# DeltaNet stage of a hybrid trunk: the k heads of both groups first, one triangular solve for all eight heads, merges by pairs

## The chip, the cores and the metric

The kernel runs on one core of a Trainium2 chip. The metric is the device time of one execution in microseconds; lower is better. Three executions of the kernel before took 1593.81, 1595.70 and 1596.45 us (median 1595.7).

## What is computed

The reference is a decoder trunk of two layers over 512 positions of width 1024. Layer 0 mixes with a gated DeltaNet, layer 1 with a Conformer convolution; behind each come a cross attention (4 heads) into 256 memory rows and a squared-ReLU MLP of width 4096, with an RMS norm ahead of each part. Only the DeltaNet stage matters here (8 heads of dimension 128; i and j run over a chunk's positions):

```python
proj = h @ w_in                                   # q, k, v, z, b, a
qkv = silu(causal_depthwise_conv(qkv, w_conv))    # width 4
q, k = l2_normalize(q) * 128 ** -0.5, l2_normalize(k)
beta = sigmoid(b);  g = -exp(a_log) * softplus(a + dt_bias);  g_cum = cumsum(g)
decay[i, j] = exp(g_cum[i] - g_cum[j])            # for i >= j
lower = strict_lower((k * beta) @ k.T * decay)
u, w = triangular_solve(eye + lower, [v * beta, k * beta * exp(g_cum)])
# over the chunks: v_new = u - w @ S;  o = q_dec @ S + (q @ k.T * decay) @ v_new
#                  S = S * exp(g_last) + k_dec.T @ v_new
out = (rms_norm(o) * out_norm * silu(z)) @ w_out
```

## The kernel before, in words

The 512 positions are cut into four blocks of 128, so that every head has four lower triangular 128x128 matrices whose inverse U is needed.

**Projections.** Each fp32 product is three matmuls of fp32r parts (L220 to L222; for z L251 to L253): a weight is split into `wh`, which ACT casts (L204), and `wl`, which DVE subtracts (L72). SyncE loads the weights in halves of 128x1024 into three buffers; three split buffers let the splits run ahead. Most tensors of 128x512 live in one pool of slots; larger ones of 128x1024 for the solve live in a pool `fsp` of three.

**The order of the work.** The stage is a list of *mains*, each 12 projection matmuls, and a table of *side steps*: `S.at(main, rank, step)` says behind which main a step is written. `DN_ORDER` sets the order of the projections. Mains 0 to 3 are the gates and the first k head; before, k of heads 0 to 3 stands at mains 4 to 9, then q at 10 to 17, z at 18 to 25, v at 26 to 33; the second group of four heads follows from 34 to 65 in the same order, and from 66 to 81 come the keys and values of the first cross attention ("K", "V"). A scheduler then builds each engine's queue from what was written. Each engine takes its queue in order.

**The steps of a head**, with the names that the profile shows:
- `decay_in`: POOL multiplies `gi` = tri_le times g (L72), ACT casts `gih` (L257), DVE subtracts `gil`. `decay`: PE sums it into `dt` (L402, L403), ACT takes the exponential (L405), POOL multiplies by `tri_le`. `gsum` (L395 to L397) is the first matmul of it.
- `ev_k`, `ev_q`, `ev_v` call `conv_head`: DVE evicts a projection to `cv`, ACT scales the first tap (L415), the other three taps are DVE multiply-adds (L75), or ACT `cvq` (L419) and a POOL add: none of k's is on POOL, one of q's, all three of v's (`CONV_K`, `CONV_Q`, `CONV_V`). Then ACT's `silu` (L426).
- `k2`: PE transposes k (`kt`, L440) and multiplies the Gram matrix (`G`, L444); ACT squares and copies (L446, L448); DVE multiplies G by the decay into `bt`, and POOL scales bt by `s_all`. `q2`, `q3`: the product of q and k (`ai`, L466) and sums of squares.
- `fs_in`: ACT copies the 32x32 diagonal blocks of bt into `DB`, four copies a head (L493).
- The solve. `fs_begin`: POOL sets `X` to the identity, DVE transposes DB into `FT`. `fs_steps`: 31 times, a product `fst` and a subtraction from X on DVE (L72); this inverts the diagonal blocks, in the free dimension and for all blocks at once. `fs_end`: transposes `TB` and `UB` (L517, L518).
- The merges make U of the whole block from the inverses of the diagonal blocks. `mg_pre`: POOL clears tiles. `mg_a`: ACT copies TB into `x0` (L537, four a head), POOL copies UB into `u0`. `mg_w` (L546) and three steps `mg_y` (L558; the last one is in `mg_end`): matmuls "mg" of PE, an ACT copy, a DVE addition.
- `norm_k`, `v2` (transposes `vt` of v, L583), then `rec`: 12 steps of the recurrence for each group of four heads; `o_gate`, `o_norm` and `head_out`, and the output projection "do".

Before, the solve is done once for each group of four heads; DB has 32 columns, of which a group fills 16, so POOL clears it first. `FS` = ((20, 9), (50, 8)) starts the solves at mains 20 and 50 and spreads them over 9 and 8 mains; `MG` = (32, 63) places the merges, `REC` = (39, 68) the recurrences.

Of the kernel before, what the change touches and what calls it, by code (L numbers as in the profile page):

```python
# [14 lines left out]
P = 128  # L15
# [25 lines left out]
def tile_trunk(ctx, tc, xT, memT, prm_d, adt_d, bdw_d, w_ab, w_kq, w_v, w_z, w_dno, w_pw1, w_pw2,  # L41
# [285 lines left out]
    class DeltaNet:  # L327
        def __init__(self, norm):
            self.n, self.xs = norm, norm.xs
            for n, s in ((64, "abt"), (32, "beta"), (32, "g"), (96, "egd"), (32, "sek"), (32, "nk"),  # L330
                         (32, "s_all"), (32, "sdec"), (32, "s_neg"), (32, "sdec_neg"), (32, "ssq"), (4, "tok")):
                setattr(self, s, keepc(n, s))
            for s in ("GI", "DtM", "KT", "Kt", "Ai", "QT", "BT", "U", "VT", "VB", "Z", "OG", "ps", "M"):
                setattr(self, s, {})
            self.DB, self.fs = {}, {}
            self.S = [None, None]
# [71 lines left out]

        def conv_head(self, ps, ti, npool):
            raw = wp.tile([P, 542], F32, tag="cv", name=nm("cv"), bufs=NCV)  # L410
            pool.memset(raw[:, 0:3], 0.0)
            tt(dve, raw[:, 3:515], ps, self.n.rb, ALU.mult)
            w = [pc("w_conv", ti * 4 + j) for j in range(4)]
            a = slot(s="cva")
            act.activation(a, raw[:, 0:512], AF.Copy, scale=w[0])  # L415
# [69 lines left out]
        def fs_in(self, h):  # L485
            gq, bt, n = h // 4, c4(self.BT[h]), h % 4 * 4
            if gq not in self.DB:
                self.DB[gq] = fsp.tile([P, 1024], F32, tag="fs", name=nm("DB"))
                pool.memset(self.DB[gq], 0.0)
            db = self.DB[gq].rearrange("p (i n) -> p i n", n=32)  # L490
            for b in range(4):
                bs = slice(32 * b, 32 * b + 32)
                act.copy(db[bs, :, n:n + 4], bt[bs, :, bs].rearrange("p c i -> p i c"))  # L493

        def fs_begin(self, gq):
# [4 lines left out]
            dve.transpose(out=FT, in_=self.DB.pop(gq))  # L500
            self.fs[gq] = FT, X

        def fs_steps(self, gq, j0, j1):
            B3, X3 = [t.rearrange("p (i j) -> p i j", j=32) for t in self.fs[gq]]
            for j in range(j0, min(j1, 31)):
# [6 lines left out]

        def fs_end(self, gq):
            X = self.fs.pop(gq)[1]
            UB = fsp.tile([P, 1024], F32, tag="fs", name=nm("UB"))
            TB = fsp.tile([P, 1024], F32, tag="fs", name=nm("TB"))
            dve.transpose(out=TB, in_=X.rearrange("p (i j) -> p j i", j=32))  # L517
            dve.transpose(out=UB, in_=X)  # L518
            self.fs[gq] = UB.rearrange("p (i n) -> p n i", n=32), TB.rearrange("p (i n) -> p n i", n=32)

# [10 lines left out]
        def mg_a(self, h):  # L531
            UBv, TBv = self.fs[h // 4]
            u0, x0, bt = self.M[h]
            n = slice(h % 4 * 4, h % 4 * 4 + 4)
            for b in range(4):
# [6 lines left out]
        def mg_w(self, h):  # L542
            u0, x0, bt = self.M[h]
            ps = psum("mg")
            for c in range(4):
                pe.matmul(c4(ps)[:, c, 0:96], bt[:, c * P:(c + 1) * P], c4(x0)[:, c, 0:96], start=True, stop=True)  # L546
            w = slot(s="w")
            act.activation(c4(w)[:, :, 0:96], c4(ps)[:, :, 0:96], AF.Copy, scale=-1.0)
            self.M[h] = u0, u0, w, 1

        def mg_y(self, h):
            u0, y, w, n = self.M[h]
            ps = psum("mg")
# [9 lines left out]
            self.M[h] = u0, y, w, n + 1  # L563

# [5 lines left out]
        def ev_v(self, h):  # L570
            self.VT[h] = self.conv_head(self.ps.pop(("v", h)), 16 + h, CONV_V)

# [533 lines left out]
    at = {}  # L1106
# [203 lines left out]
CONV_K, CONV_Q, CONV_V = 0, 1, 3  # L1310
DEC1 = (37, 43)
K2 = (13, 12, 16, 17, 43, 44, 47, 46)
Q2 = (16, 18, 20, 21, 46, 48, 48, 51)
FS = ((20, 9), (50, 8))
MSTEP = (0, -1)
MG = (32, 63)
V2 = (4, 3)
MGAIN = 4
HO = 76
REC = (39, 68)  # L1320
MEM = 53
# [97 lines left out]
```

## Time and profile before

| | us |
|---|---|
| median of three executions | 1595.7 |
| profiled execution | 1596.47 |
| its span | 1594.8 |
| PE busy in it | 1545.7 |
| DVE busy | 919.2 |
| ACT busy | 661.9 |
| POOL busy | 275.3 |

The span is the time from the first to the last recorded instruction; the mean granted clock of TensorE was 0.983. A line of the timeline has start, duration, engine, source line, operation, "out<-in" by the program's names, the shape and, in brackets, the idle time just before with what ended it. In a table of windows each engine's busy time comes with its count, then the granted clock (PEclk, 1 is full), the DMA engines' busy share and GB/s. Matmuls overlap, so their durations sum to more than their starts lie apart.

### The profile page before, as it was taken

Reading aid. Unit: us, or ns where it says so; the run is one execution under the profiler, and the core shown is the slowest. Engines: PE = TensorE matmul, PEld = TensorE weight load, DVE = VectorE, ACT = ScalarE, POOL = GpSimd, SP = SyncE. Lnnn points to the kernel's source line nnn. Section 1 sums busy time; section 2 is a strip of 40 time slices with the busy share of each in tenths; the row PEclk is TensorE's granted clock in tenths of the full one; section 3 lists DMA queues with packets and bytes.
Section 4 is the critical chain, followed back from the end, with each engine's and each line's share of the span. In section 5 each row is a group of like instructions: output and inputs, shape, how many; then the busy total and the mean of one; then the engine's idle time right before and its main releaser. Section 6 shows DMA issues by size and latency. Waiting matters only on the chain.

```text
span 1594.8 us, 19977 instructions
## 1 busy us (share of the span) xinstructions
PE 1545.7 (97%) x7864; PEld 1310.7 (82%) x7864; DVE 919.2 (58%) x1304; ACT 661.9 (42%) x1014; POOL 275.3 (17%) x314
## 2 busy tenths in 40 slices
PE   9998997899999999999999999999999999999997
PEld 6777886798888888888888889888888888888897
DVE  6886878566455444343445599974445443444443
ACT  6656573745344443241324321264434442323332
POOL 1526333502111100000021316102112000000002
PEclk9999999799999999999999999999999999999999
DMA  5121113153222222322322422252213223322321
GB/s 179 67 76 57 53 40 106 43 183 106 93 66 66 86 100 93 106 93 92 104 95 93 145 80 78 76 170 95 79 40 106 93 92 98 101 93 96 103 93 54
DMA packets 47614, 147.09 MB, mean 92 GB/s; under 512 B 6304, under 2 KB 11040, under 8 KB 47520
## 3 DMA queue, kind: packets, MB, share of 16 engines
q1 hardware_dynamic: 47520, 145.81, 27.5%
q8 instruction: 62, 1.02, 0.3%
q14 instruction: 32, 0.26, 0.0%
HBM read 142.38 MB, written 2.10 MB: 91 GB/s over the span
## 4 chain that ended last, share of the span: by engine, by line
PE 83%; DVE 8%; ACT 3%; POOL 2%; issue 2%; SPq 1%; DMA 1%; DVEq 0%; ACTq 0%; POOLq 0%
PE dn L220 7%; PE dn L221 7%; PE dn L222 7%; PE up L220 7%; PE up L221 7%; PE up L222 7%; DVE ca L75 4%; PE q L220 2%; PE xo L221 2%; PE q L221 2%; PE q L222 2%; PE xo L222 2%; PE xo L220 2%; PE h L221 2%; PE pw L220 2%; PE pw L221 2%
## 5 line engine op out<-in xcount | busy, mean ns | idle before, releaser
L204 ACT CAST wh<-raw 128x1024 fp32r<-128x1024 f32 x248 | 260.3, 1051 | 706.8 <-PE dn L221 191.4
L72 DVE TENSOR_TENSOR wl<-raw,wh 128x1024 fp32r<-128x1024 f32 x248 | 313.8, 1266 | 126.6 <-ACT wh L204 120.7
L220 PE MATMUL up<-xh,wh 128*128 128x512 f32 x512 | 200.2, 391 | 0.0
L222 PE MATMUL up<-xh,wl 128*128 128x512 f32 x512 | 199.2, 389 | 0.0
L221 PE MATMUL up<-xl,wh 128*128 128x512 f32 x512 | 199.2, 389 | 0.0
L220 PE MATMUL dn<-uh,wh 128*128 128x512 f32 x448 | 174.3, 389 | 0.0
L221 PE MATMUL dn<-ul,wh 128*128 128x512 f32 x448 | 174.3, 389 | 0.0
L222 PE MATMUL dn<-uh,wl 128*128 128x512 f32 x448 | 174.3, 389 | 0.0
L72 DVE TENSOR_TENSOR h<-dn,h 128x512 f32<-128x512 f32 x56 | 41.9, 748 | 170.4 <-PE dn L222 170.4
L75 DVE SCALAR_TENSOR_TENSOR rl<-up,rb 128x512 f32<-128x512 f32 x64 | 44.2, 691 | 156.9 <-PE up L222 156.9
L72 POOL TENSOR_TENSOR tap<-ident,prm 128x512 f32<-128x512 f32 x45 | 60.7, 1380 | 330.8 <-PE up L222 263.8
L220 PEld LDWEIGHTS up<-xh,wh 128*128 128x128 f32 x512 | 96.1, 188 | 20.4 <-issue 0.5
L221 PEld LDWEIGHTS up<-xl,wh 128*128 128x128 f32 x512 | 96.1, 188 | 20.2 <-issue 0.5
L222 PEld LDWEIGHTS up<-xh,wl 128*128 128x128 f32 x512 | 96.1, 188 | 20.1
L222 PEld LDWEIGHTS dn<-uh,wl 128*128 128x128 f32 x448 | 84.1, 188 | 17.5
L220 PEld LDWEIGHTS dn<-uh,wh 128*128 128x128 f32 x448 | 84.1, 188 | 17.5
L221 PEld LDWEIGHTS dn<-ul,wh 128*128 128x128 f32 x448 | 84.1, 188 | 17.4
L72 POOL TENSOR_TENSOR sq<-sq,sq 128x512 f32<-128x512 f32 x30 | 49.9, 1664 | 252.5 <-ACT sq L295 167.8
L75 DVE SCALAR_TENSOR_TENSOR ca<-x,prm,ca 128x512 f32<-128x512 f32 x90 | 81.8, 910 | 2.1
L220 PE MATMUL h<-xh,wh 128*128 128x512 f32 x192 | 77.6, 404 | 1.9 <-ACT xh L288 1.9
L221 PE MATMUL h<-xl,wh 128*128 128x512 f32 x192 | 76.0, 396 | 0.6 <-DVE xl L75 0.6
L222 PE MATMUL h<-xh,wl 128*128 128x512 f32 x192 | 75.7, 394 | 0.0
(322 smaller groups left out, 3211.1 us busy)
## 6 DMA issues: line engine op xcount, KB each, us to landing
raw<-w_up SPq DMA_DIRECT2D x64, 512.0 KB, 3.4
raw<-w_dn SPq DMA_DIRECT2D x64, 512.0 KB, 3.4
raw<-w_pw SPq DMA_DIRECT2D x24, 512.0 KB, 3.6
raw<-w_kq SPq DMA_DIRECT2D x16, 512.0 KB, 3.7
raw<-w_k SPq DMA_DIRECT2D x16, 512.0 KB, 3.7
raw<-w_vv SPq DMA_DIRECT2D x16, 512.0 KB, 3.6
raw<-w_q SPq DMA_DIRECT2D x16, 512.0 KB, 3.5
raw<-w_o SPq DMA_DIRECT2D x16, 512.0 KB, 3.5
```

Source lines behind the costliest of these rows:

```text
L72: e.tensor_tensor(out=o, in0=a, in1=b, op=op)
L75: dve.scalar_tensor_tensor(out=o, in0=a, scalar=s, in1=b, op0=op0, op1=op1)
L204: act.copy(h, raw)
L220: pe.matmul(ps, wh, xh, start=first, stop=False)
L221: pe.matmul(ps, wh, xl, start=False, stop=False)
L222: pe.matmul(ps, wl, xh, start=False, stop=last)
```

## The change

All eight k heads are projected first (mains 2 to 17), then v of the first group at 18 to 25, q at 26 to 33, z at 34 to 41, and v, q, z of the second group at 42 to 65. There is one DB, whose 32 columns the eight heads fill (so it isn't cleared), and one solve, from main 23 over 9 mains. The decays of heads 4 to 7 come at mains 11 to 15 in place of 37 to 45. The merges go by pairs of heads, a pair every three mains from main 32, each with its own `mg_pre` one main ahead. In the merges w is written over bt, and y over x0. The v heads of the second group are convolved in the pool of the solve, whose tiles are free by then. `K2`, `Q2`, `V2` and `HO`, which place the steps named alike, move with their inputs. The diff, cut:

```diff
@@ DeltaNet.__init__
-            self.DB, self.fs = {}, {}
+            self.DB = self.fs = None
@@ conv_head, ev_v
-        def conv_head(self, ps, ti, npool):
+        def conv_head(self, ps, ti, npool, a=None):
...
-            a = slot(s="cva")
+            a = slot(s="cva") if a is None else a
...
-            self.VT[h] = self.conv_head(self.ps.pop(("v", h)), 16 + h, CONV_V)
+            a = None
+            if h >= 4:
+                if h % 2 == 0:
+                    self.VP = fsp.tile([P, 1024], F32, tag="fs", name=nm("VT"))
+                a = self.VP[:, h % 2 * 512:h % 2 * 512 + 512]
+            self.VT[h] = self.conv_head(self.ps.pop(("v", h)), 16 + h, CONV_V, a)
@@ fs_in, fs_begin, fs_end
-            gq, bt, n = h // 4, c4(self.BT[h]), h % 4 * 4
-            if gq not in self.DB:
-                self.DB[gq] = fsp.tile([P, 1024], F32, tag="fs", name=nm("DB"))
-                pool.memset(self.DB[gq], 0.0)
-            db = self.DB[gq].rearrange("p (i n) -> p i n", n=32)
+            bt, n = c4(self.BT[h]), h * 4
+            if self.DB is None:
+                self.DB = fsp.tile([P, 1024], F32, tag="fs", name=nm("DB"))
+            db = self.DB.rearrange("p (i n) -> p i n", n=32)
...
-            dve.transpose(out=FT, in_=self.DB.pop(gq))
-            self.fs[gq] = FT, X
+            dve.transpose(out=FT, in_=self.DB)
+            self.fs = FT, X
...
@@ mg_a, mg_w, mg_y
-            n = slice(h % 4 * 4, h % 4 * 4 + 4)
+            n = slice(h * 4, h * 4 + 4)
...
-            w = slot(s="w")
+            w = bt
...
-                y = slot(s="y")
+                y = x0
...
@@ the table of side steps
+    f0, nf = FS
+    S.at(f0, 5, D.fs_begin)
+    for i in range(nf):
+        S.at(f0 + i, 6, D.fs_steps, i * 31 // nf, (i + 1) * 31 // nf)
+    S.at(f0 + nf, 0, D.fs_end)
+    for h in range(8):
+        S.at(MGP[h], 5, D.mg_pre, h)
+        S.at(MG[h], 1, D.mg_a, h)
+        for j, f in enumerate((D.mg_w, D.mg_y, D.mg_y, D.mg_end)):
+            S.at(MG[h] + MGLAG + j, 1, f, h)
     for gq in range(2):
-        f0, nf = FS[gq]
-        S.at(f0, 5, D.fs_begin, gq)
-        for i in range(nf):
-            S.at(f0 + i, 6, D.fs_steps, gq, i * 31 // nf, (i + 1) * 31 // nf)
-        S.at(f0 + nf, 0, D.fs_end, gq)
-        S.at(f0 + 1, 7, D.norm_k, gq)
-        for i in range(4):
-            h = 4 * gq + i
-            m = MG[gq] + i * MSTEP[gq] // 2
-            S.at(m, 1, D.mg_a, h)
-            S.at(f0 + nf - 4 + i, 5, D.mg_pre, h)
-            for j, f in enumerate((D.mg_w, D.mg_y, D.mg_y, D.mg_end)):
-                S.at(m + 1 + j, 1, f, h)
+        S.at(f0 + 1 + gq, 7, D.norm_k, gq)
         for c in range(4):
-            S.at(max(at["v", 4 * gq + 3] + V2[gq], f0 + nf), 3, D.v2, gq, c)
+            S.at(at["v", 4 * gq + 3] + V2[gq], 3, D.v2, gq, c)
@@ the numbers
-DN_ORDER = (("k", 0), ("q", 0), ("z", 0), ("v", 0), ("k", 1), ("q", 1), ("z", 1), ("v", 1))
+DN_ORDER = (("k", 0), ("k", 1), ("v", 0), ("q", 0), ("z", 0), ("v", 1), ("q", 1), ("z", 1))
...
-DEC1 = (37, 43)
+DEC1 = (11, 13)
...
-FS = ((20, 9), (50, 8))
-MSTEP = (0, -1)
-MG = (32, 63)
+FS = (23, 9)
+MGP = (31, 31, 34, 34, 37, 37, 40, 40)
+MG = (32, 32, 35, 35, 38, 38, 41, 41)
+MGLAG = 1
...
-REC = (39, 68)
+REC = (41, 66)
```

How this moves instructions. **POOL**, behind the first decays. The names: gi_442 and dt_515 to dt_545 are of heads 0 to 3. Before:

```order
L72 TENSOR_TENSOR gi_442<-tri_le,g 128x512
L72 TENSOR_TENSOR dt_515<-dt_515,tri_le 128x512
L72 TENSOR_TENSOR dt_521<-dt_521,tri_le 128x512
L72 TENSOR_TENSOR dt_539<-dt_539,tri_le 128x512
L72 TENSOR_TENSOR dt_545<-dt_545,tri_le 128x512
L411 MEMSET cv_1198 128x3
L72 TENSOR_TENSOR cva_551<-cva_551,cvq_553 128x512
```

and in the changed order, where gi_557, gi_563 and dt_626 are of heads 4 to 7 and bt_602 is a scaled Gram matrix:

```order
L72 TENSOR_TENSOR dt_515<-dt_515,tri_le 128x512
L72 TENSOR_TENSOR dt_521<-dt_521,tri_le 128x512
L72 TENSOR_TENSOR dt_539<-dt_539,tri_le 128x512
L72 TENSOR_TENSOR gi_557<-tri_le,g 128x512
L72 TENSOR_TENSOR dt_545<-dt_545,tri_le 128x512
L411 MEMSET cv_1011 128x3
L72 TENSOR_TENSOR gi_563<-tri_le,g 128x512
L411 MEMSET cv_1065 128x3
L72 TENSOR_TENSOR bt_602<-bt_602,s_all 128x512
L72 TENSOR_TENSOR dt_626<-dt_626,tri_le 128x512
```

The products gi of heads 4 to 7, which were far behind, now stand between and behind the dt products of heads 0 to 3.

**ACT**, around the last copies into DB. Before, the first solve's last copies (DB_666, of the fourth head's bt_775):

```order
L575 ACT_TABLE_LOAD
L575 ACTIVATE nk<-sek 128x16
L426 ACT_TABLE_LOAD
L426 ACTIVATE cva_793<-cva_793 128x512
L493 COPY DB_666<-bt_775 32x32x4 x4
L204 CAST wh_859<-raw_699 128x1024
L578 ACTIVATE s_neg<-s_all 128x16
L578 ACTIVATE sdec_neg<-sdec 128x16
L468 ACTIVATE sqq_914<-cva_793 128x512
L204 CAST wh_938<-raw_805 128x1024
L204 CAST wh_995<-raw_857 128x1024
```

In the changed order the last copies are of the seventh and eighth head, and the first v heads' taps (cva_1014, cvq_1016 and so on) stand among them:

```order
L426 ACT_TABLE_LOAD
L426 ACTIVATE cva_941<-cva_941 128x512
L492 COPY DB_721<-bt_929 32x32x4 x2
L415 ACTIVATE cva_1014<-cv_1011,prm 128x512
L419 ACTIVATE cvq_1016<-cv_1011,prm 128x512
L419 ACTIVATE cvq_1019<-cv_1011,prm 128x512
L419 ACTIVATE cvq_1022<-cv_1011,prm 128x512
L492 COPY DB_721<-bt_929 32x32x4 x2
L204 CAST wh_1031<-raw_880 128x1024
L426 ACTIVATE cva_1014<-cva_1014 128x512
L492 COPY DB_721<-bt_989 32x32x4 x4
L204 CAST wh_1095<-raw_956 128x1024
```

Behind these rows FT can be transposed; before, that takes 16 copies of four heads, now 32 of eight.

**PE**, at the merges. Before, the first group's merges (mg_1322 and on, with x0 and bt as operands) stand in one row of four heads:

```order
L222 MATMUL h_1264<-xh_166,wl_1145 128x512
L546 MATMUL mg_1322<-x_218_1044,bt_627 128x96 x4
L546 MATMUL mg_1329<-x_227_1080,bt_592 128x96 x4
L546 MATMUL mg_1336<-x_238_1126,bt_740 128x96 x4
L546 MATMUL mg_1343<-x_247_1163,bt_775 128x96 x4
L220 MATMUL h_1370<-xh_138,wh_1214 128x512
L221 MATMUL h_1370<-xl_140,wh_1214 128x512
```

and the second group's far behind, next to the sum mssq of the memory's squares:

```order
L546 MATMUL mg_2615<-x_530_2449,bt_1961 128x96 x4
L719 MATMUL mssq_2622<-msq_2426,ones 128x256 x2
L546 MATMUL mg_2666<-x_510_2369,bt_1844 128x96 x4
L546 MATMUL mg_2673<-x_519_2407,bt_2022 128x96 x4
L558 MATMUL mg_2680<-u_529_2448,w_2620 96x96 x4
L220 MATMUL h_2720<-xh_138,wh_2528 128x512
```

In the changed order the first pair (mg_1481, mg_1487) stands behind the last q projection of group 0, and the second pair (mg_1650, mg_1656) behind the first z steps; the first pair's further steps and z projections lie between the two pieces:

```order
L222 MATMUL h_1402<-xh_166,wl_1235 128x512
L545 MATMUL mg_1481<-x_302_1369,bt_649 128x96 x4
L545 MATMUL mg_1487<-x_304_1377,bt_602 128x96 x4
L466 MATMUL ai_1493<-cva_1360,cva_418 128x128 x4
L251 MATMUL z_1512<-wh_1297,xh_138 128x512
...
L557 MATMUL mg_1638<-x_302_1369,bt_649 32x32 x4
L557 MATMUL mg_1644<-x_304_1377,bt_602 32x32 x4
L545 MATMUL mg_1650<-x_342_1555,bt_712 128x96 x4
L545 MATMUL mg_1656<-x_344_1563,bt_764 128x96 x4
L480 MATMUL ssq_1662<-ones,sqq_1617 128x1 x4
L251 MATMUL z_1514<-wh_1398,xh_146 128x512
```

The eight heads' merges are spread over the mains 33 to 45, with projections between the steps, and nothing of a second group is left behind them.

More of the change, by code (lines that the diff above doesn't have):

```diff
@@ L493, in fs_in, with fs_begin @@
                 act.copy(db[bs, :, n:n + 4], bt[bs, :, bs].rearrange("p c i -> p i c"))
-        def fs_begin(self, gq):
+        def fs_begin(self):
             X = fsp.tile([P, 1024], F32, tag="fs", name=nm("X"))
@@ L499, in fs_begin, with fs_steps @@
             FT = fsp.tile([P, 1024], F32, tag="fs", name=nm("FT"))
-            dve.transpose(out=FT, in_=self.DB.pop(gq))
-            self.fs[gq] = FT, X
-        def fs_steps(self, gq, j0, j1):
-            B3, X3 = [t.rearrange("p (i j) -> p i j", j=32) for t in self.fs[gq]]
+            dve.transpose(out=FT, in_=self.DB)
+            self.fs = FT, X
+        def fs_steps(self, j0, j1):
+            B3, X3 = [t.rearrange("p (i j) -> p i j", j=32) for t in self.fs]
             for j in range(j0, min(j1, 31)):
@@ L511, in fs_steps, with fs_end @@
                 tt(dve, X3[:, w:32, 0:w], X3[:, w:32, 0:w], t3, ALU.subtract)
-        def fs_end(self, gq):
-            X = self.fs.pop(gq)[1]
+        def fs_end(self):
+            X = self.fs[1]
             UB = fsp.tile([P, 1024], F32, tag="fs", name=nm("UB"))
@@ L546, in mg_w @@
                 pe.matmul(c4(ps)[:, c, 0:96], bt[:, c * P:(c + 1) * P], c4(x0)[:, c, 0:96], start=True, stop=True)
-            w = slot(s="w")
+            w = bt
             act.activation(c4(w)[:, :, 0:96], c4(ps)[:, :, 0:96], AF.Copy, scale=-1.0)
-            self.M[h] = u0, u0, w, 1
+            self.M[h] = u0, u0, w, x0, 1
         def mg_y(self, h):
-            u0, y, w, n = self.M[h]
+            u0, y, w, x0, n = self.M[h]
             ps = psum("mg")
@@ L1310 @@
 CONV_K, CONV_Q, CONV_V = 0, 1, 3
-DEC1 = (37, 43)
-K2 = (13, 12, 16, 17, 43, 44, 47, 46)
-Q2 = (16, 18, 20, 21, 46, 48, 48, 51)
-FS = ((20, 9), (50, 8))
-MSTEP = (0, -1)
-MG = (32, 63)
-V2 = (4, 3)
+DEC1 = (11, 13)
+K2 = (13, 12, 14, 15, 16, 17, 19, 20)
+Q2 = (30, 31, 33, 35, 54, 56, 58, 60)
+FS = (23, 9)
+MGP = (31, 31, 34, 34, 37, 37, 40, 40)
+MG = (32, 32, 35, 35, 38, 38, 41, 41)
+MGLAG = 1
+V2 = (8, 7)
 MGAIN = 4
-HO = 76
-REC = (39, 68)
+HO = 73
+REC = (41, 66)
 MEM = 53
```

6 lines of the change are left out of this document (3 added, 3 removed).

## The prediction

> **What bounds the kernel now.** I read the page's first lines, then the table of time windows cut at three events of the program, then the list of PE's waits, then the timelines of the engines that those waits name.
>
> ```profile
> span 1594.8 us, 19977 instructions
> PE 1545.7 (97%) x7864; PEld 1310.7 (82%) x7864; DVE 919.2 (58%) x1304; ACT 661.9 (42%) x1014; POOL 275.3 (17%) x314
> ...
> PE 83%; DVE 8%; ACT 3%; POOL 2%; issue 2%; SPq 1%; DMA 1%; DVEq 0%; ACTq 0%; POOLq 0%
> ```
>
> PE is busy for 97% of the span, so all but some 50 us of the kernel is matrix work, and 83% of the chain that ended last is PE. A change that leaves every matmul in place can only move the rest: the idle time of PE and the time in which PE ran at less than its full clock. Both have to be looked for in the DeltaNet stage, the only one that is changed. Four PE events divide it.
>
> ```profile
> 44.07 0.31 PE L395 MATMUL gsum<-g,ones 128*128 128x32 f32 x2
> ...
> 136.41 7.04 PE L546 MATMUL mg<-x,bt 128*128 128x96 f32 x32 [4.93 <-ACT x L537]
> ...
> 373.73 0.39 PE L220 MATMUL do<-oh,wh 128*128 128x512 f32 x1
> ...
> 374.41 0.39 PE L220 MATMUL do<-oh,wh 128*128 128x512 f32 x1
> ```
>
> The columns are start, duration, engine, line and operation. At 44.07 comes the first matmul of the decays, at 136.41 the first merge (of heads 0 to 3), at 373.73 the output projection. The second group's first merge is at 280.58 and comes up below as the end of a wait. Up to 44.07 and behind 373.73 PE has the same rows in both programs, so the change decides one number: when "do" starts. The windows between the events:
>
> ```profile
> core 0: us, PE busy (x) PEld busy (x) DVE busy (x) ACT busy (x) POOL busy (x), PEclk, DMA share, GB/s
> 44.10:136.40 92.30, 81.06 (x403) 67.14 (x402) 77.58 (x130) 54.71 (x90) 38.72 (x54) 0.98 0.23 75
> 136.40:280.60 144.20, 129.16 (x761) 112.34 (x761) 108.88 (x195) 82.86 (x148) 58.81 (x90) 0.94 0.19 63
> 280.60:373.70 93.10, 89.39 (x612) 81.88 (x613) 59.30 (x86) 55.15 (x98) 24.28 (x32) 0.89 0.34 114
> ...
> 44.10:92.40 48.30, 41.98 (x217) 34.61 (x216) 36.31 (x50) 34.02 (x58) 24.38 (x35) 0.96 0.20 66
> 280.60:310.50 29.90, 26.18 (x145) 23.08 (x146) 15.44 (x20) 25.59 (x51) 21.10 (x30) 0.67 0.11 36
> ```
>
> In the first window PE stands idle for 92.30 - 81.06 = 11.2 us, in the second for 15.0, in the third for 3.7. The clock column adds a second loss: (1 - 0.94) x 144.2 = 8.7 us in the second window and (1 - 0.89) x 93.1 = 10.2 us in the third, nearly all of the latter in its first 29.9 us (0.67 of full clock). Behind the first merge the stage loses 15.0 + 3.7 + 8.7 + 10.2 = 37.6 us. The waits say what for:
>
> ```profile
> PE mg L546 <- POOL msq L72: 11.2, 1, 11.2
> PE mg L546 <- ACT x L537: 5.3, 2, 4.9
> ```
>
> The columns are total, times and longest. The 11.2 us end with the first merge of the second group. The view names POOL's sum of squares, but that stands on another tile; what the merge needs is the second solve, whose last DVE transpose ends late (a solve takes 41 us, below). So two waits for a solve, and the slow clock behind each, are what this stage loses.
>
> **The change, first part: when the one solve can start.** It starts with the transpose FT, which needs the diagonal blocks of all eight heads, copied by ACT (DB, 4 copies a head). ACT takes its queue in order, so its queue up to the last DB copy is what I sum. Before, FT started at 92.49.
>
> ```profile
> L493 ACT COPY DB<-bt 32x128 f32<-32x128 f32 x16 | 6.7, 418 | 4.8 <-POOL bt L72 4.6
> L204 ACT CAST wh<-raw 128x1024 fp32r<-128x1024 f32 x4 | 4.2, 1040 | 1.9 <-PE h L221 1.9
> L415 ACT ACTIVATE cva<-cv,prm 128x512 f32<-128x512 f32 x5 | 3.6, 725 | 0.1
> L426 ACT ACTIVATE cva<-cva 128x512 f32<-128x512 f32 x5 | 3.2, 631 | 5.8 <-DVE cva L75 5.7
> L419 ACT ACTIVATE cvq<-cv,prm 128x512 f32<-128x512 f32 x4 | 2.9, 714 | 0.0
> L426 ACT ACT_TABLE_LOAD x2 | 2.6, 1283 | 0.0
> L446 ACT ACTIVATE sqk<-kt 128x512 f32<-128x512 f32 x4 | 2.4, 589 | 0.0
> L448 ACT COPY kt<-kt 128x512 f32<-128x512 f32 x4 | 2.3, 572 | 0.0
> L405 ACT ACTIVATE dt<-dt 128x512 f32<-128x512 f32 x4 | 2.0, 593 | 0.0
> L257 ACT CAST gih<-gi 128x512 fp32r<-128x512 f32 x3 | 1.8, 616 | 2.1 <-POOL gi L72 2.1
> ```
>
> These are ACT's groups between 44.1 and 92.4; the number behind the comma is the mean of one in ns. The first row where both orders still agree on ACT is the cast that ends at 51.98:
>
> ```profile
> 50.93 1.05 ACT L204 CAST wh<-raw 128x1024 fp32r<-128x1024 f32 x1 [1.91 <-PE h L221]
> ```
>
> From there to the last DB copy the changed order holds 32 DB copies (13.4 us), 5 casts (5.2), 8 squares and 8 copies of kt (9.3), 7 table loads (9.0), 8 exponentials (4.7), 4 casts of gi (2.5), 7 first taps (5.1), 7 silu (4.4) and 6 further taps (4.3): 58 us as recorded. Records overlap: the groups of the window sum to 36.5 us where its row says 34.02 busy, so 58 become 54. With no idle time FT starts at 52 + 54 = **106**; with ACT as busy as in that window (34.02 of 48.30) at 52 + 54/0.704 = **129**. What I see between: in the changed order the POOL products gi of heads 4 to 7 stand behind the dt products of heads 0 to 3, and ACT's cast of each gi waits at the head of its queue.
>
> ```profile
> L72 POOL TENSOR_TENSOR gi<-tri_le,g 128x512 f32<-128x512 f32 x3 | 5.4, 1828 | 0.0
> ...
> 53.16 6.37 POOL L72 TENSOR_TENSOR dt<-dt,tri_le 128x512 f32<-128x512 f32 x4 [4.80 <-ACT dt L405]
> ```
>
> One dt product takes 6.37 / 4 = 1.59 us; the first gi, behind three, ends at 53.16 + 3 x 1.59 + 1.83 = 59.8, when ACT has come to its cast at 51.98 + 0.73 + 4 x 0.59 = 55.1: 4.7 us of wait. The second pair meets two dt products and no third; I take 3.5. Behind the cast stand the taps, the silu and the DB copies, so all are late by it. With 2 us for smaller waits (bt on POOL): 52 + 54 + 8 + 2 = **116**.
>
> **Second part: how long the solve takes.** The number of DVE steps is that of one solve of before: the tile had 32 columns, of which 16 were used. The rows are from DVE's timeline, from the window of the steps' tile fst (us, DVE busy and count, clock, DMA share, GB/s) and from DVE's groups, of the solve and (taps) of the stretch ahead of it.
>
> ```profile
> 92.49 1.25 DVE L500 STREAM_TRANSPOSE FT<-DB 128x1024 f32<-128x1024 f32 x1 [1.70 <-ACT DB L493]
> 115.81 0.39 DVE L72 TENSOR_TENSOR X<-X,fst 128x231 f32<-128x231 f32 x1
> 117.67 1.37 DVE L72 TENSOR_TENSOR X<-X,fst 128x220 f32<-128x220 f32 x1
> 131.96 1.93 DVE L517 STREAM_TRANSPOSE TB<-X 128x1024 f32<-128x1024 f32 x1
> ...
> 92.00:136.40 44.40, 26.18 (x62) 1.00 0.25 83
> ...
> L72 DVE TENSOR_TENSOR wl<-raw,wh 128x1024 fp32r<-128x1024 f32 x7 | 8.5, 1212 | 0.0
> L72 DVE TENSOR_TENSOR cv<-h,rb 128x512 f32<-128x512 f32 x4 | 2.7, 676 | 0.1
> L75 DVE SCALAR_TENSOR_TENSOR cva<-cv,prm,cva 128x512 f32<-128x512 f32 x11 | 11.8, 1074 | 3.4 <-POOL cva L72 3.2
> ```
>
> Before, it ran from 92.49 to 133.89, 41.4 us. The window row counts the steps alone: 62 in 26.18 us. The changed order puts beside them 5 weight splits (6.1), 4 conv evictions (2.7), 6 taps (6.4) and 2 products of q, priced as evictions (1.4), and there are FT and TB (3.2) and some 0.035 us between two steps (2.2): **48 us**. So TB ends at 116 + 48 = 164. Then ACT copies the blocks into x0, and the first merge can go:
>
> ```profile
> 135.02 6.72 ACT L537 COPY x<-TB 32x128 f32<-32x128 f32 x16
> ```
>
> That is 0.42 each. The merge of the first head needs 4 of them, 1.7 us: **166**, with 154 + 2 = 156 and 179 as bounds. PE itself isn't late by then: its work up to there grows by about 5.3 us (below).
>
> The two X steps above stand 2 us apart and take 0.39 and 1.37: the second began beside a POOL add. The Trainium skill, page "SBUF — State Buffer", section "Who interferes with whom", says that DVE's second pair of ports is shared with GpSimd under an exclusive lock; the two rows agree, though on average a step took 26.18 / 62 = 0.42. By that rule the three further POOL adds beside the new solve cost 1 us each, and the sum would be 3 us higher, 1592. The terms above leave it out.
>
> **Third part: from the first merge to the output projection.** Before: 373.73 - 136.41 = 237.3 us. Two things come off.
>
> ```profile
> 55.02 1.06 PE L444 MATMUL G<-cva 128*128 128x128 f32 x8
> 55.83 0.47 PE L220 MATMUL h<-xh,wh 128*128 128x512 f32 x1
> ...
> 315.72 1.97 PE L583 MATMUL vt<-ident,cva 128*128 128x128 f32 x16
> ```
>
> Work moved ahead of the first merge: both orders have 276 projection matmuls there. The change adds 8 decays of 512 columns at 0.227 (three do matmuls in 374.41 - 373.73), 16 Gram matmuls at 0.203 (four, as 8 records, from 55.02 to 55.83), and 16 + 16 transposes at about 0.11 (16 in 1.97 less the drain of the last): 1.8 + 3.2 + 3.5. It takes away 8 q·k matmuls and 8 sums at 0.2: 3.2. Net **5.3 us**.
>
> Losses that go: of the 37.6 us, the second solve, its 11.2 us of wait and the half clock behind it have no place in the new order, because all U are there long before the second group's recurrence. What remains: a half clock behind the new first wait (3.4 us, as 136.4 to 143.2 had it), some 2 us in the recurrences, and 1.3 us elsewhere, because a pair's merge steps now have one projection step of 2.7 us between them. That is 6.7 in place of 37.6, **30.9** off; the bounds of what remains are 3 (little but the clock) and 13 (with the 9.9 us that the clock lost in 280.6 to 310.5). So 237.3 - 5.3 - 30.9 = 201.1, and do starts at 166 + 201.1 = 367.1, **6.6 us sooner**. DVE has more room than before behind the merge, by one solve. The moved norm_k, the reused w and y tiles and the v heads in another pool I take at nothing: they add no instruction to PE or ACT, and the copy into w waits for the matmuls that read bt anyway, since it reads their result. The reuse frees slots, so it may gain too; I allow 3 us either way, about PE's idle time in the third window.
>
> The profiled execution is 1596.47 us, 1.7 above its span, and 0.8 above the median 1595.7. 1596.5 - 6.6 = 1589.9; against the median **1589**.
>
> **The rivals.** (a) *ACT is the whole bound and hardly waits.* For: after 52 its queue is dense in the new order. Against: ACT was idle for 30% of the first half. FT at 106 to 110 gives 1579 to 1583. (b) *The long wait before the first merge keeps PE slow.* PE now stands for about 30 us around the merge, far more than before; behind the second merge the clock was 0.67 for 29.9 us, 9.9 us lost, against 3.4 in my sum. Then 6.5 of the 6.6 us are gone: about 1595.6, no change. The Trainium skill, "TensorE: Matmul & The Clock Gate", Part 1, has full rate return after about 3.4 us of sustained work; the stretch behind 136.4 agrees, the 29.9 us behind 280.6 don't, where PE had gaps. By that rule this rival would not come. (c) *The solve starts too late: slower.* Its place is ACT's queue ahead of the last DB copy. Every us there moves the first merge and with it do by one. The gain is gone when FT starts at 116 + 6.6 = 122.6. With ACT's idle share of before it starts at 129: 6.4 us slower, 1602. For it: new waits of ACT for POOL, and 8 heads in one queue. Against: fewer q and z rows of ACT stand between. That the change doesn't make one solve can be left out: the order has one FT, one TB and one UB.
>
> **How the numbers follow.** Forecast (1583 to 1592.5) 0.40; bigger gain (a) 0.17; no change (b) 0.19; slower (c) 0.24. About 0.2%, 3.2 us, is what a measurement can tell from no change. Faster is 0.40 + 0.17 = 0.57, same 0.19, slower 0.24. The low end is (a) with 3 us of remaining losses in place of 6.7: 1577; the high end is (c) with 1 us more: 1603.
>
> **What would show it.** FT near 116, TB's end near 164, first merge near 166 and do near 367; PE without the 11.2 us wait; DVE busy some 30 us less than 919.2; a PE wait of over 20 us around the first mg, on ACT x or on the casts. FT beyond 122 with do late says (c); a low clock for more than 7 us behind the merge says (b). If PE waits in the merges or recurrences for more than 7 us, my third part is wrong.

## The result, and the profile after

**No change.** Twelve executions of the changed kernel have a median of 1595.85 us (1594.75 to 1597.31) beside 1596.03 us (1592.50 to 1597.30) for twelve of the kernel before: a ratio of 1.0004, 95% interval 0.9997 to 1.0011 (estimated from all executions of both, here and below, so not the quotient of the two medians). The forecast was 6.6 us less. The single executions of either kernel lie up to 5 us apart, and their mean granted clock goes with them (the kernel before: 1592.6 us at 0.987, 1597.0 at 0.983, in one set of runs), so of all that follows only differences over some 2 us are read from times; the rest is read from one trace of each kernel, between two of its own events.

The changed kernel's page, its first lines:

```profile
span 1594.1 us, 19919 instructions
PE 1543.3 (97%) x7864; PEld 1304.3 (82%) x7864; DVE 893.1 (56%) x1239; ACT 663.3 (42%) x1014; POOL 273.4 (17%) x310
```

DVE does 26 us less, as one solve less should make it. PE is as busy as it was, and as long. The four events in its timelines, of PE and DVE:

```profile
44.43 0.31 PE L395 MATMUL gsum<-g,ones 128*128 128x32 f32 x2
...
169.28 1.10 PE L545 MATMUL mg<-x,bt 128*128 128x96 f32 x8 [2.10 <-issue]
...
373.60 0.39 PE L220 MATMUL do<-oh,wh 128*128 128x512 f32 x1
```

```profile
116.47 1.25 DVE L499 STREAM_TRANSPOSE FT<-DB 128x1024 f32<-128x1024 f32 x1 [0.65 <-ACT DB L492]
...
165.30 2.06 DVE L516 STREAM_TRANSPOSE TB<-X 128x1024 f32<-128x1024 f32 x1
```

FT starts where the working put it (116), TB ends at 167.4 in place of 164, the first merge comes at 169.3 in place of 166, and "do" at 373.6 in place of 367: 0.1 us before where it was. So the stage's two parts, ahead of and behind the first merge, changed as forecast in kind: the first merge is 33 us later and all that follows it 33 us shorter. The windows show both:

```profile
core 0: us, PE busy (x) PEld busy (x) DVE busy (x) ACT busy (x) POOL busy (x), PEclk, DMA share, GB/s
...
116.50:167.40 50.90, 33.52 (x138) 26.96 (x137) 44.84 (x86) 21.39 (x34) 14.71 (x19) 0.77 0.18 61
44.40:169.30 124.90, 96.15 (x444) 77.66 (x442) 100.66 (x169) 81.55 (x137) 60.88 (x90) 0.88 0.17 55
169.30:373.60 204.30, 202.15 (x1333) 179.03 (x1333) 120.56 (x181) 112.96 (x198) 66.04 (x88) 0.99 0.29 95
...
116.50:143.00 26.50, 18.27 (x66) 13.85 (x65) 25.04 (x42) 15.95 (x25) 9.51 (x11) 0.87 0.29 97
143.00:169.30 26.30, 15.26 (x73) 13.16 (x73) 21.71 (x47) 7.30 (x14) 5.84 (x10) 0.68 0.07 21
```

Behind the first merge PE is idle for 2.2 us of 204.3 at 0.99 of its clock: hardly anything is left to gain there, and the 11.2 us wait is gone. Ahead of it PE is idle for 28.75 us (before: 11.2). In the last 26.3 us ahead of the merge it is busy for 15.3 at 0.68 of the clock. PE's waits, the largest three of the whole execution (the third lies behind "do"), say for whom:

```profile
PE ai L466 <- ACT cva L426: 12.1, 2, 8.6
PE h L222 <- DVE wl L72: 3.9, 2, 2.4
PE K L222 <- DVE wl L72: 3.8, 2, 3.6
```

The longest of PE's waits are not for the solve. PE stands for the silu of two q heads, whose products with k ("ai") are next in its queue. And DVE, in the middle of the solve, stands for PE. DVE's waits between 90 and 172, the first two:

```profile
DVE wl L72 <- ACT wh L204: 8.5, 3, 4.3
DVE ssq L81 <- PE ssq L480: 3.8, 1, 3.8
```

The chain of work, followed back from the first merge, crosses over (start, duration, what):

```profile
150.37 0.39 DVE fst L72
150.76 0.66 DVE cva L75
151.42 0.30 DVE X L72
151.72 0.67 DVE cva L75
...
152.42 0.64 ACT cva L426
...
153.10 2.07 PE ai L466 x8
155.17 1.50 PE ssq L480 x8
156.67 0.64 PE h L220
...
161.85 0.79 PE ssq L480 x8
162.63 1.80 PE vt L587 x16
...
167.19 2.10 issue
169.28 0.77 PE mg L545 x5
```

A tap of q lies among the solve's steps in DVE's queue (151.72); ACT's silu waits for it, PE's "ai" for the silu (8.6 us). PE has stood long enough for its clock to fall, so the 12 projection matmuls that follow take 5.2 us (156.67 to 161.85) in place of 2.8. Behind them comes the sum of squares of q, and for that DVE stops between two solve steps, from 158.8 to 162.7. **PE waits for DVE's queue, and DVE's queue then waits for PE.**

Where did the gain go? Every microsecond from "gsum" to "do" is one of three: PE idle, the half of its busy time at half clock that is lost, or the work at full clock. Worked out from PE's records and the clock of each trace:

| from gsum to do | elapsed | PE idle | lost at half clock while busy | work at full clock |
|---|---|---|---|---|
| before, to the first merge | 92.3 | 11.2 | 1.7 | 79.4 |
| before, from there to do | 237.3 | 18.8 | 13.9 | 204.7 |
| changed, to the first merge | 124.9 | 28.8 | 9.9 | 86.2 |
| changed, from there to do | 204.3 | 2.2 | 1.7 | 200.5 |

Lost time fell by 28.8 us behind the merge and grew by 25.7 ahead of it; the work grew by 2.6 in all. PE has the same 1775 matmul records in both kernels; why they take 2.6 us more was not taken apart.

### The profile page after: what moved, and what is told of

The parts are those of the page before. It is cut to its first block, busy times and chain, and to the rows that moved or that the text cites. A ratio compares the mean times of both kernels' runs of the same rounds, so it can differ in the third digit from the quotient of the medians.

```text
span 1594.1 us, 19919 instructions
## 1 busy us (share of the span) xinstructions
PE 1543.3 (97%) x7864; PEld 1304.3 (82%) x7864; DVE 893.1 (56%) x1239; ACT 663.3 (42%) x1014; POOL 273.4 (17%) x310
## 4 chain that ended last, share of the span: by engine, by line
PE 82%; DVE 11%; ACT 3%; issue 2%; POOL 1%; DMA 0%; DVEq 0%; SPq 0%; POOLq 0%; ACTq 0%
PE dn L220 7%; PE dn L222 7%; PE dn L221 7%; PE up L220 7%; PE up L222 7%; PE up L221 7%; DVE ca L75 4%; PE q L220 2%; PE xo L221 2%; PE q L222 2%; PE q L221 2%; PE xo L222 2%; PE xo L220 2%; DVE wl L72 2%; PE pw L220 2%
## 5 line engine op out<-in xcount | busy, mean ns | idle before, releaser
L220 PE MATMUL h<-xh,wh 128*128 128x512 f32 x192 | 81.2, 423 | 6.1 <-ACT wh L204 3.7
```

What stands on the lines that cost most here:

```text
L220: pe.matmul(ps, wh, xh, start=first, stop=False)
```

## The experiments

Theory A was that PE and DVE wait for each other ahead of the first merge, and that the lost time can be had back if PE has other work there. Its rivals are named in the expectations. "From gsum" means that the start of "gsum" in the same trace is subtracted; in the changed kernel TB then ends at 122.9, the first merge is at 124.9 and do at 329.2.

**1. The sums of squares of q later** (e1, and once more beside the changed kernel, e14 and e13).

```diff
-        S.at(Q2[h] + 1, 3, D.q3, h)
+        S.at(Q2[h] + 1 if h >= 4 else 36 + h // 2, 3, D.q3, h)
```

> The changed kernel, with the sums of squares of q of heads 0 to 3 written behind mains 36 and 37 in place of 31 to 36. Theory A (PE and DVE wait for each other: DVE, in the middle of the solve, stands 3.8 us for PE's ssq, while PE stands for taps that are queued behind solve steps): the end of TB moves from 167.4 to about 163.5, the first merge from 169.3 to 166 or 167, where PE itself comes free; the 8 sums (1.6 us) come later instead; do starts 0.8 to 2.2 us sooner, 1594 to 1595. Theory B (the 3.8 us are slack of DVE that something else would fill): TB ends at 167 and the time stays at 1595.9 or rises.

> The kernel with the sums of squares of q later, once more. Its trace had do 1.8 us sooner after the first decay than the changed kernel's, but its median of 11 runs was not faster. If the gain is real and the spread hid it: 1 to 2.5 us below the changed kernel beside it. If PE's slow clock gives it back in most executions: within 1 us of it or above.

> The changed kernel once more, as the measure for the two runs beside it: 1595 to 1597, within 0.1% of the kernel before.

The three events in the trace of e1:

```profile
43.35 0.31 PE L395 MATMUL gsum<-g,ones 128*128 128x32 f32 x2
...
160.57 2.05 DVE L516 STREAM_TRANSPOSE TB<-X 128x1024 f32<-128x1024 f32 x1
...
164.39 1.10 PE L545 MATMUL mg<-x,bt 128*128 128x96 f32 x8 [2.10 <-issue]
```

TB ends at 119.3 from gsum, 3.7 us sooner, the first merge comes 3.8 sooner (121.0), and do 1.8 sooner (327.4) in the one trace and 2.1 in the other (the sums themselves now come behind the merge, where the work grows from 200.5 to 202.5 us): DVE's wait for PE was 3.7 us of the solve, as theory A has it, and theory B falls. The time doesn't settle it. The ratio to the kernel before was 1.0005 (0.9996 to 1.0014) in the first set and 0.9999 (0.9990 to 1.0008) in the second, where the changed kernel beside it had 1.0006 (0.9998 to 1.0015); the medians were 1596.8, then 1594.3 beside 1596.4. Executions of this kernel reach from 1592.6 to 1597.9. Whether the 2 us arrive in the median stays open.

**2. The q products behind the merge, the merges later, and both.** These three are read together: e2, e5 and e3 (e12 is e3 again).

```diff
-Q2 = (30, 31, 33, 35, 54, 56, 58, 60)
+Q2 = (36, 37, 38, 39, 54, 56, 58, 60)
```

> The changed kernel, with the q products and sums of heads 0 to 3 behind the first merges (mains 36 to 39 in place of 30 to 35). Theory A: PE no longer waits 12.1 us for q's silu and reaches the first merge some 15 us early, but waits there for TB, which ends near 164; the q work (3.2 us) now follows the merge. The two cancel: do at 373 to 374, 1595.5. Theory C (PE's waits for q's taps are what makes the first merge late): the time falls by 8 us or more, below 1588.

```diff
-MGP = (31, 31, 34, 34, 37, 37, 40, 40)
-MG = (32, 32, 35, 35, 38, 38, 41, 41)
+MGP = (35, 35, 38, 38, 41, 41, 44, 44)
+MG = (36, 36, 39, 39, 42, 42, 45, 45)
...
-REC = (41, 66)
+REC = (45, 66)
```

> The changed kernel, with merges and first recurrence four mains later, as in the run that gained, but with the q products left at mains 30 to 35. Theory A (before the merge PE stands for q's taps, not for TB, so a later merge alone gives it nothing to do): 1593 to 1596.5, and PE's two waits of 12 us for q's silu stay. Rival (the merges' place alone made the gain): 1589 or less.

The third has the second diff, and Q2 = (37, 38, 39, 40, 54, 56, 58, 60).

> The changed kernel, with the merges and the first recurrence four mains later and the q products behind the first merge. Theory A: while the solve ends, PE does four more mains (11 us) that it did behind the merge before; with 3.2 us of q work moved the other way do starts about 8 us sooner: 1588. Theory D (DVE is full from 116 to 167, and each split and eviction that PE asks for there pushes the solve's end back): TB ends at 168 or later and the gain is 4 us or less, 1592 to 1596.

> The kernel with merges four mains later once more, as the measure for the two runs beside it: 1585.5 to 1588.5.

| q products | merges at main 32 | merges four mains later |
|---|---|---|
| ahead of the merge | 1595.85, ratio 1.0004 (0.9997 to 1.0011) | 1598.29, 1.0024 (1.0015 to 1.0032) |
| behind it | 1596.56, 1.0007 (0.9998 to 1.0016) | 1586.56, 0.9947 (0.9934 to 0.9959) |

The repeat of the last gave 1586.40, 0.9946 (0.9934 to 0.9958). Neither edit alone gains; both together gain 9 us. PE's waits of the first two, the largest row of each:

```profile
PE mg L545 <- ACT x L536: 20.2, 1, 20.2
```

```profile
PE ai L466 <- ACT cva L426: 12.0, 2, 8.6
```

With only the q products moved, PE stands 20.2 us for the solve instead of 12 for q; with only the merges moved it still stands 12.0 us for q, and since the solve is over by then, the later merges come behind still more work: the first is at 137.4 from gsum, do 1.9 us later than in the changed kernel, and the time is 1.8 us above the range expected. With both, PE does z projections while DVE ends the solve:

```profile
116.50:143.00 26.50, 21.46 (x91) 17.08 (x90) 25.02 (x44) 15.94 (x26) 9.32 (x10) 0.87 0.23 82
143.00:166.30 23.30, 20.66 (x91) 16.43 (x89) 22.55 (x43) 8.51 (x14) 6.65 (x10) 1.00 0.19 68
...
43.40:166.40 123.00, 105.71 (x489) 84.96 (x487) 102.60 (x166) 83.89 (x139) 61.80 (x90) 0.94 0.18 65
166.40:362.90 196.50, 190.34 (x1288) 169.93 (x1288) 118.48 (x183) 110.42 (x196) 66.67 (x88) 0.98 0.27 94
```

These are that kernel's windows, cut at its own first merge (166.36) and do (362.90). From 143 to the merge PE is busy for 20.7 of 23.3 us at full clock, where the changed kernel had 15.3 of 26.3 at 0.68. The merge comes 123.0 from gsum, hardly sooner than 124.9, but 100.2 us of work stand ahead of it in place of 86.2. From gsum to do PE is idle for 23.5 us in place of 30.9 and loses 8.8 at half clock in place of 11.6. More moved ahead than the four mains of the expectation: in PE's queue 77 z matmuls stand there, over six mains of 12, because the scheduler builds the queue. Theory A holds; theory C (q's taps alone) falls by e2, which gains nothing, and theory D (DVE too full for the splits that PE then asks for) by e3, where TB ends at 121.6, not later.

**3. How many mains later?** Five (e8) and two (e15) in place of four.

```diff
-MG = (36, 36, 39, 39, 42, 42, 45, 45)
+MG = (37, 37, 40, 40, 43, 43, 46, 46)      # e8; MGP, Q2 and REC[0] move along
...
+MG = (34, 34, 37, 37, 40, 40, 43, 43)      # e15; likewise
```

> The kernel of the run that gained, with merges, q products and first recurrence one more main later (five in all). PE waits 2.7 us at its first merge there, so one main of 2.8 us fills that and no more: 0 to 2 us sooner, 1584.5 to 1586.5. If every main that goes ahead of the merges is worth its own 2.8 us: 1583.5 or less.

> As the run that gained 9 us, but with merges, q products and first recurrence two mains later than in the changed kernel in place of four. If each main that PE can do while the solve ends is worth its 2.8 us: halfway between the 1596.5 of q products alone and 1586.5, so 1590 to 1592.5. If the gain comes all at once, when PE no longer stands long enough for the clock to fall: 1587 or less, or 1595 or more.

Five: 1589.09, ratio 0.9966 (0.9953 to 0.9978), some 2 to 3 us slower than four, and slower than either branch expected. PE is idle as long as with four (23.7 us from gsum to do beside 23.5); the time lost at half clock is 12.4 us beside 8.8 and, in the trace of the repeat, 10.9. Two: 1585.83, ratio 0.9937 (0.9924 to 0.9950), the fastest of all, though its interval overlaps that of four. Neither run answers the question of main by main or all at once: in the queues that the scheduler built, PE's first merge stands behind the same 487 matmul records from gsum on with two, four and five, 100 us of work. What differs is only what follows, so it is not shown either that a fifth main ahead of the merges has nothing to fill.

**4. The start of the solve.** The decays of heads 4 to 7 earlier (e4):

```diff
-DEC1 = (11, 13)
+DEC1 = (9, 10)
```

> The changed kernel, with the decays of heads 4 to 7 prepared at mains 9 and 10 in place of 11 and 13, so that most of POOL's gi products stand ahead of the dt products. If the 8 us that I put on ACT's and PE's waits for gi are real, FT starts at 108 to 111 in place of 116.5 and do follows it by most of that: 1588 to 1591. If the copies into DB wait for the k projections' own pace instead, FT stays within 2 us of 116.5 and the time within 2 us of 1595.9.

It is slower: 1599.60, ratio 1.0028 (1.0017 to 1.0039). ACT's waits between 44 and 118, the first three of the changed kernel and the first five of this one:

```profile
ACT gih L257 <- POOL gi L72: 9.5, 5, 4.2
ACT wh L204 <- PE h L221: 1.9, 1, 1.9
ACT cva L426 <- POOL cv L411: 1.1, 1, 1.1
```

```profile
ACT DB L492 <- POOL bt L72: 4.1, 2, 2.5
ACT cva L426 <- DVE cva L75: 4.1, 2, 3.5
ACT gih L257 <- POOL gi L72: 2.1, 2, 1.4
ACT wh L204 <- PE h L221: 1.9, 1, 1.9
ACT cva L426 <- POOL cva L72: 1.6, 1, 1.6
```

The waits for gi go, as expected, from 9.5 to 2.1 us. Their place is taken by waits for bt, whose first product on POOL now stands behind all eight dt products and, when these are done, still waits 3.0 us for `s_all` from DVE, and by waits for taps. FT starts at 75.1 from gsum, 3.1 later than the changed kernel's 72.0, the first merge 3.4 later and do 3.4 later. So both expected branches are wrong, and the run shows two things: the wait that I priced was real but not one to be had, and a later start of the solve moves do nearly one for one.

**5. POOL beside the solve.** First 16 further POOL products without an input from the solve (e7), then 16 that read what a step has just written (e9); both leave the results as they are.

```diff
                 tt(dve, X3[:, w:32, 0:w], X3[:, w:32, 0:w], t3, ALU.subtract)
+                if 8 <= j < 24:
+                    tt(pool, tri_gt, tri_gt, ones, ALU.mult)                     # e7
...
+                    tt(pool, self.junk, tmp[:, 0:P], tmp[:, 0:P], ALU.mult)      # e9
```

> The changed kernel, with 16 further POOL multiplications (128x128, a constant by ones, which leaves it as it is) beside the solve's steps 8 to 23. If a POOL instruction that reads SBUF holds up the DVE step that meets it, as the steps of 1.3 us beside the taps suggest, the 62 steps take 2 to 6 us more than the 28.4 of the changed kernel, and do comes later by that. If those long steps had another cause, they take 28 to 29.

> The changed kernel, with 16 further POOL multiplications of 128x128, each of which reads the product that a solve step has just written (steps 8 to 23) into a scrap tile, so that they cannot run ahead of the solve as those of the run before did. If a POOL instruction that reads SBUF holds up the DVE step that meets it, the 62 steps take 31 us or more in place of 28.4, and TB and do come 3 us or more later, about 1599. If the steps of 1.3 us beside the taps had another cause, the steps take 28 to 29 us and do moves by less than 1 us.

In e7 the scheduler put the 16 far ahead, at 44 to 58, so it says nothing of the solve's steps (28.3 us). It delays FT instead, by 5.0 us from gsum; the first merge moves by 5.5 and do by 3.9: again nearly one for one (1599.02, one execution). In e9 they lie beside the solve. The window row of the steps' tile has DVE's time for it, 62 steps, and POOL's for the 16:

```profile
92.00:176.00 84.00, 27.86 (x62) 9.72 (x16) 0.82 0.17 57
```

27.9 us, where the changed kernel's 62 steps took 28.4: with 9.7 us of POOL beside them the sum is no longer than it was. Single steps show why:

```profile
148.40 0.49 DVE L72 TENSOR_TENSOR fst<-FT,X 128x240 f32<-128x240 f32 x1
148.92 0.41 DVE L72 TENSOR_TENSOR X<-X,fst 128x240 f32<-128x240 f32 x1
```

A step beside a POOL product of 128 columns takes 0.07 to 0.09 us more (0.49 beside 0.40 without), two of them 0.20 more, some 1 us in all, while the steps beside the taps' POOL adds of 512 columns take 1.3. Those adds were there already, and two of them, beside which steps of the changed kernel took 1.36 and 0.89 us, no longer hold a step up here; so the level sum is in part a cancellation. Still the expectation of 31 us was wrong: a short POOL instruction costs a step little. The time is 1597.50 (ratio 1.0016, 1.0006 to 1.0026); TB and do come 2.3 us later from gsum, though the steps don't. DVE's waits between 90 and 172 have a row that the changed kernel's lack:

```profile
DVE cva L75 <- POOL cva L72: 2.3, 2, 1.2
```

Two taps of q on DVE wait for POOL's adds, which now stand behind the new products, and the solve's next steps stand behind these taps in DVE's queue. PE's largest wait, for q's silu, grew from 12.1 to 14.7 us with them.

**6. The kernel before with its second merges later** (e6).

```diff
-MG = (32, 63)
-HO = 76
-REC = (39, 68)
+MG = (32, 66)
+HO = 79
+REC = (39, 71)
```

> The kernel before, with the second group's merges and recurrence and the heads' output three mains later, so that three K steps (1.5 us each) can stand ahead of the merges. If the 11.2 us before the second merge are a wait that other work can fill, 4 to 5 us of them go, and some of the slow clock with them: 1589 to 1592. If K's own inputs, the normed memory, come no sooner, the wait only changes its name: 1594 to 1597.

It is slower than either branch expected: 1601.14, ratio 1.0036 (1.0024 to 1.0048), and the 11.2 us wait has only another name. PE's largest two waits:

```profile
PE mssq L719 <- POOL msq L72: 11.2, 1, 11.2
PE mg L546 <- ACT x L537: 9.4, 2, 4.9
```

So PE stands for msq's product on POOL as well, which the prediction had put aside. In the kernel before it can't be told which of the two ended the wait: the second group's first merge, at 280.58, reads x and bt, and the third of its copies of x ends at 280.49, msq's product at 280.55. Both were late for the same reason. TB had ended at 273.4, 7 us ahead of the merge. ACT's timeline there:

```profile
273.51 0.41 ACT L537 COPY x<-TB 32x128 f32<-32x128 f32 x1 [1.82 <-DVE TB L517]
279.02 0.63 ACT L426 ACTIVATE cva<-cva 128x512 f32<-128x512 f32 x1 [5.11 <-POOL cva L72]
279.67 1.25 ACT L537 COPY x<-TB 32x128 f32<-32x128 f32 x3
```

After one copy ACT comes to a silu, and waits 5.1 us for POOL's taps, which stand among POOL's copies of u; the product of msq stands behind them. Of the 11.2 us only some 4 were the solve.

**7. Two more steps from the best version** (e10, e11; both start from the merges four mains later).

```diff
-V2 = (8, 7)
+V2 = (12, 7)        # e10
...
-FS = (23, 9)
+FS = (23, 7)        # e11
```

> The kernel with merges four mains later (1586.6), with the transposes of v four mains later too. Two evictions vb (1.4 us of DVE) leave the solve's stretch, so TB ends about 1.4 us sooner; PE's work ahead of the merge falls by 1.7 us and its wait there stays near 2.7 us. If the solve's end still sets do: 1585 to 1586. If PE's own work does by now: 1586 to 1588.

> The kernel with merges four mains later (1586.6), with the solve's steps spread over 7 mains in place of 9, so that they stand ahead of one split, one eviction and two taps that they shared DVE with. If the solve's end sets do, TB ends 2 to 4 us sooner and the time falls to 1583.5 to 1585.5. If the splits and evictions that now come later hold PE up by as much, 1586 to 1588.

Both do to the solve what they should: TB ends 1.5 and 2.6 us sooner from gsum than in the version beside them (121.5). Both are slower than it, and than either branch expected: 1589.87 (ratio 0.9965, 0.9953 to 0.9977) and 1591.38 (0.9987, 0.9972 to 1.0003). In e10 PE has 2.6 us less work ahead of the merge and stands 5.0 us there in place of 2.7; its clock falls just then (half of it from 164.3 to 171.1), and do comes 2.7 later. In e11, whose trace is of one of the longer executions (1596.34 us), the taps that the solve steps have overtaken come behind TB, and ACT's copies of TB stand behind a silu that waits for them. ACT's timeline:

```profile
165.71 0.63 ACT L426 ACTIVATE cva<-cva 128x512 f32<-128x512 f32 x1 [4.23 <-DVE cva L75]
...
167.47 1.67 ACT L536 COPY x<-TB 32x128 f32<-32x128 f32 x4
```

TB had ended at 162.7, so 4.8 us are lost on ACT, and the first merge comes 125.1 from gsum beside 123.0. In this version an earlier end of the solve alone no longer pays. Its shorter executions, of 1589.9 to 1591.5 us, have no trace, so how much of this they share is not shown.

## Why the prediction was wrong, point by point

Two steps of the sum failed, each about half of the 6.5 us that are missing: the second part took DVE's waits for PE at nothing (3.8 us in the solve), and the third part took off losses of which 4.6 us were counted twice.

- **What bounds the kernel: right**, that only idle time and slow clock can move, and where. **Its size was wrong by counting twice.** I added PE's idle time and the windows' clock loss to 37.6 us. But while PE waited for the second merge its clock was already down: in the windows of before around its two waits PE is not busy at all at 0.50 and 0.73.

```profile
273.00:280.50 7.50, 0.00 (x0) 0.00 (x0) 2.12 (x3) 1.85 (x4) 5.57 (x8) 0.50 0.07 26
298.80:302.00 3.20, 0.00 (x0) 0.00 (x0) 3.20 (x3) 3.20 (x8) 3.00 (x4) 0.73 0.00 0
```

  Half of 7.5 and 0.27 of 3.2, together 4.6 us, were in both terms. The right sum is 33.0 (worked out from the records, as in the table above, 18.75 + 13.88 = 32.6). That the first of these waits was all for the solve was wrong too: run 6 leaves the solve some 4 us of the 11.2.
- **First part, the start of the solve: right.** FT at 116.47 for 116, ACT's waits for gi behind 52 at 4.2, 0.6 and 2.7 us for my 8.2. That the wait could be taken away was not claimed, and run 4 shows that it can't be so simply.
- **Second part, the solve: 50.9 us for 48.** The failed step is the sum's silent assumption that DVE, once started, only has its own queue to work off. It lacked the 3.8 us in which DVE waits for PE's ssq; run 1 takes them away, and TB with them. The steps took 28.4 us in place of 26.2; the taps 4.5 in place of 6.4, so these two nearly cancel. Two evictions vb of 0.7 us each stood beside the steps too, and were not in the sum.
- **"PE itself isn't late by then": true of the merge, but with the wrong reason.** PE came free 2.1 us ahead of the merge. The prediction checked only that PE's work was small, not what its queue waits for: q's silu held PE for 12.1 us, and PE's late sums then held the solve. The PE wait of over 20 us that was forecast around the first merge did not come; it comes, with 20.2 us, once the q products are out of the way (e2).
- **Third part: 204.3 us for 201.1.** The losses that go were 28.8 for 30.9: 4.6 us less by the double count, 2.8 more since only 3.9 us of loss remain behind the merge where I left 6.7. The work that moved ahead brought 4.2 us for my 5.3.
- **The sum.** The first merge comes 3.3 us later than forecast (gsum 0.4, the solve 2.9) and the rest takes 3.2 longer: the whole 6.5 us between -6.6 and -0.1. No part had the wrong sign; two errors near 3 us ate the difference of two numbers near 30 (36.2 us less behind the first merge, 29.6 more ahead of it).
- **The rivals.** The time came out as in (b), but not by it: behind the merge the clock is 0.99 and 1.7 us are lost, not 9.9. Rival (c)'s rule, that a later FT moves do one for one, holds in runs 4 and 5 (3.1 to 3.4, 5.0 to 3.9), yet FT was not late. The low clock was ahead of the merge, where neither looked.

## What to carry to other kernels

When a change gathers work on one engine, list for the stretch that it fills what the other engines' queues wait for there: a step of another head that sits between the gathered steps can stop PE, and PE's next result can stop the gathered steps. A wait that is removed is worth its length only if the engine has other work at that place in its queue, so the place of the consumer has to move together with that of what stands ahead of it: here each edit alone gave 0 or a loss, both together 9 us (1586 us, ratio 0.9946, with the merges four mains later; 1586, 0.9937, with two). What a table of places asks for has to be read back from the queue that the scheduler builds: two, four and five mains gave the same rows ahead of the first merge. And lost time is counted once: idle time, or slow clock while busy, not both.

## What the runs showed of the hardware

- The granted clock costs a part of the time beside the waits: from gsum to do the changed kernel lost 11.6 us at half clock and 30.9 idle. In its last 26.3 us ahead of the merge PE was busy for 58% of the time in pieces, and had 0.68 of its clock; busy for 89% of the last 23.3 us, with the merges four mains later, it had 1.00. The Trainium skill, "TensorE: Matmul & The Clock Gate", Part 1, puts the fall at about 3.4 us of idleness. In these traces every half-clock stretch from gsum to do lasts 3.4 us or a multiple (6.8 at 130.8, 17.1 at 144.5 in the changed kernel), which fits that length; but PE need not be idle all through it: in the 3.4 us ahead of the changed kernel's four falls it was busy, at full clock, for 1.1, 0.7, 1.1 and 1.9 us. Nor is one such length always enough for the return: from 136.4 on the kernel before ran merges at half clock for 6.8 us, a stretch that the prediction had counted as agreeing.
- One kernel's executions fall into groups by that clock: of twelve executions of e11 eight took 1589.9 to 1591.5 us at 0.987 to 0.988, four took 1596.3 to 1600.0 at 0.981 to 0.984. The one trace of e11 is of the smaller group, so a profile of one execution can stand for the wrong one.
- DVE and POOL hold each other up by the length of the instruction that is in the way: a solve step took 1.27 to 1.37 us in place of some 0.2 to 0.4 beside POOL adds of 1.3 us, but 0.07 to 0.09 us more, twice 0.20, beside POOL products of 0.4. The Trainium skill, "SBUF — State Buffer", "Who interferes with whom", gives the shared ports as an exclusive lock; by it I had put 3 us on three further adds, and the steps took 2.25 us more. The rule agrees with the long adds; as a price for each POOL instruction 1 us is too high, by run 5.
